# The front of a conformer, RWKV-7 and feed-forward layer: TensorE's order written out, and the output products of the two branches exchanged

## The chip, the core and the metric

The kernel runs on one core of one Trainium2 chip. TensorE (PE, with the weight loads PEld) multiplies, VectorE (DVE), ScalarE (ACT) and GpSimd (POOL) work on whole tiles, and SyncE (SP) issues the DMAs. The metric is the device time of one execution in microseconds, and lower is better. The profile is that of one execution.

## The reference

A layer with D = 1024 channels and T = 512 positions. One input product feeds three parts: a conformer convolution, an RWKV-7 recurrence with 16 heads of 64, and two gates.

```
h = modulate(rms_norm(x, g_norm1), shift1, scale1)        # shift, scale, gate: silu(c) @ w_ada
u_conv, u_rwkv, u_gate = split(h @ w_in)
z = depthwise_conv31(za * sigmoid(zb)); y_conv = silu(layer_norm(z)) @ w_pw + b_pw
u = u + mix * (u_prev - u); r, k, v, xw, xa, xg = split(u)
decay = exp(-exp(w_log(tanh(xw) @ w2)));  a = sigmoid(a0 + xa @ a2);  kk = normalised(k * k_k)
scan:  S = S * decay + (S @ -kk) (kk * a)^T + v k^T;  y = S @ r
y_rwkv = ((group_norm(y) + bonus(r, k, v)) * g) @ w_o
x = x + gate1 * ((g_conv * y_conv + g_rwkv * y_rwkv) @ w_out)
out = x + gate2 * (relu(modulate(rms_norm(x)) @ w_ff1)**2 @ w_ff2)
```

## The kernel before

**Dense blocks.** Everything is held with channels on partitions and the 512 positions along a tile. A large product goes by blocks of 128 output channels. `wload` brings the 512 KB of weights (`raw`), ACT casts them to a high part `wH` (L215), POOL makes the low part `wL = raw - wH` (L216), and the block is 24 matmuls of 128x512: for each of 8 chunks of the contraction wH by the high activations, wH by the low ones, wL by the high ones (L223, L224, L225). `raw`, `wH` and `wL` have two buffers each, and the accumulators `mm` three. The front has 52 blocks of `w_in` (k, r and v of the 8 RWKV blocks, six pairs for the convolution, 16 gates), then 8 of `w_pw` and 8 of `w_o`; `w_out` and the two feed-forward products come after and are not touched.

**RWKV.** The 16 heads go in four groups of two blocks (four heads). A group has these parts:
- `group_k` and `group_prep`: from k the low-rank products `pw`/`pa`, the norms `ss`/`rn`, the decay's exponentials `Pt` and `Pi` (L606, L610, behind an activation-table load), `decay_k` (the row norms spread by PE in `prn`, the normalised k `kkn`, kkn·a and the corrected k `kp`, both made by POOL but for two blocks, and `BK`), then r and v, and `products` (transposes `bkt`, Gram products `pG`, the masked `G` of L666, the values `UV`).
- `group_solve`: 31 dependent steps on DVE, each a product `tm` and a sum `Y` (L721, L723), with copies by ACT ahead (L712) and transposes behind (L729, L731); `group_solve2` finishes it on PE (`sW`, `sX`).
- `group_chain`: 8 steps that depend on one another. In each PE gives `ch<-S,AR` and `ch<-UV,G` (L767, L769), ACT copies F (L772), PE gives `ch<-F,G` (L776), ACT and DVE copy one half of UV each (L778, L779), PE gives `ch<-UV,bkT` (L784), and DVE makes `sp` and the next state `S` (L791, L792). Products `Y` (L799, L801) go beside it.
- `group_post`: the group norm of Y and its output.

**Convolution.** Each of 8 channel blocks is 31 weighted sums, one on ACT and 30 on DVE (L145, "taps" below), some 240 taps of 128x512.

**What sets the order.** The program is written part after part, and the scheduler issues by priority. The table `FORWARD` moves the priority of a section by a number of steps for each group, `WINDOWS` says which convolution and gate blocks are programmed around a group's solve, `after_dense` and `amid` tie small products to the last dense block or to a place in it, and `conv_taps` of later blocks may issue from the end of the solve. So each dense matmul goes where the priorities and ready times of the scheduler's model put it. Behind the front the norm of the convolution is programmed in the last group's window, `silu` behind it, then the `w_pw` blocks, then the `w_o` blocks.

## Time and profile before

| | |
|---|---|
| median of 3 runs | 1145.9 us (1145.41 to 1153.32) |
| profiled execution | 1150.57 us, span of the trace 1148.8 us |
| mean granted TensorE clock | 0.969 of full speed |
| busy share of the span | PE 93%, PEld 71%, DVE 67%, ACT 43%, POOL 37% |
| instructions | PE 6290, DVE 1145, ACT 805, POOL 237 |

A busy PE is a PE with matmuls in flight: the small products of a chain count as busy for their whole latency, so 93% says little of what the front could give. The stages of the front are told apart by the starts of `sW` (end of a group's solve) and the end of the chain.

### The profile page before, as it was taken

What the parts mean: (1) busy time and instruction counts of PE and PEld (TensorE: products, weight loads), DVE (VectorE), ACT (ScalarE), POOL (GpSimd) and SP (SyncE); (2) the same over time, 40 slices, a digit from 0 to 9 for tenths busy, and PEclk for the clock granted to TensorE, in tenths of its full rate; (3) what the DMA queues carried; (4) which work ended last, traced back from release to release, by engine and by line L of the source; (5) the groups of instructions that cost most, each with busy time, mean ns of one, the idle gap of its engine ahead of it and who ended that gap; (6) DMA issues with size and microseconds to landing.
All of it is one profiled execution on the core that took longest, in us unless ns stands there. A gap on an engine that the chain in (4) does not pass through costs nothing.

```text
span 1148.8 us, 16008 instructions
## 1 busy us (share of the span) xinstructions
PE 1066.7 (93%) x6290; PEld 818.6 (71%) x6290; DVE 765.2 (67%) x1145; ACT 494.8 (43%) x805; POOL 429.5 (37%) x237
## 2 busy tenths in 40 slices
PE   6898999998799989999979999998999999999997
PEld 5675776666566767667656777886888888888886
DVE  5878787789877898688845649788613612522545
ACT  5555534646155473365566412334413322422331
POOL 4744242243222334125431234453444444444441
PEclk9999799998899999999978999999999999999998
DMA  9622142112321125112636779952333333333332
GB/s 321 217 71 69 47 138 75 51 52 73 99 91 51 42 69 175 48 47 65 202 106 195 232 243 335 284 158 67 92 95 107 93 92 94 107 93 92 98 101 76
DMA packets 188922, 136.73 MB, mean 119 GB/s; under 512 B 5424, under 2 KB 162480, under 8 KB 188848
## 3 DMA queue, kind: packets, MB, share of 16 engines
q1 hardware_dynamic: 188848, 135.73, 38.4%
q8 instruction: 49, 0.80, 0.3%
q14 instruction: 25, 0.20, 0.1%
HBM read 121.55 MB, written 14.16 MB: 118 GB/s over the span
## 4 chain that ended last, share of the span: by engine, by line
PE 65%; DVE 19%; ACT 6%; DMA 5%; issue 3%; POOL 2%; SPq 0%; DVEq 0%; ACTq 0%; POOLq 0%
PE mm L223 16%; PE mm L224 16%; PE mm L225 16%; DVE acc L145 4%; PE pG L663 2%; ACT wH L215 1%; PE Y L801 1%; DMA adaw<-in_w_ada_dram 1%; PE Y L799 1%; PE ch L767 1%; PE ch L776 1%; DVE t2k L251 1%; PE ch L784 1%; DVE t2k L1022 1%; POOL wL L216 1%
## 5 line engine op out<-in xcount | busy, mean ns | idle before, releaser
L216 POOL TENSOR_TENSOR wL<-raw,wH 128x1024 fp32r<-128x1024 f32 x142 | 341.7, 2406 | 592.9 <-ACT wH L215 503.6
L223 PE MATMUL mm<-b,wH 128*128 128x512 f32 x720 | 292.0, 406 | 4.1 <-ACT cv L516 2.9
L225 PE MATMUL mm<-b,wL 128*128 128x512 f32 x720 | 291.0, 404 | 3.7 <-POOL wL L216 2.9
L224 PE MATMUL mm<-b,wH 128*128 128x512 f32 x720 | 291.2, 404 | 2.2 <-DVE b L1032 2.1
L215 ACT CAST wH<-raw 128x1024 fp32r<-128x1024 f32 x142 | 149.1, 1050 | 290.7 <-PE mm L224 238.9
L145 DVE SCALAR_TENSOR_TENSOR acc<-z,vt,acc 128x512 f32<-128x512 f32 x232 | 173.1, 746 | 1.8
L223 PEld LDWEIGHTS mm<-b,wH 128*128 128x128 f32 x720 | 136.9, 190 | 36.4 <-issue 3.5
L225 PEld LDWEIGHTS mm<-b,wL 128*128 128x128 f32 x720 | 137.0, 190 | 36.0 <-POOL wL L216 3.7
L224 PEld LDWEIGHTS mm<-b,wH 128*128 128x128 f32 x720 | 137.0, 190 | 33.5 <-DVE b L1032 3.5
L224 PE MATMUL mm<-g,wH 128*128 128x512 f32 x328 | 128.2, 391 | 1.2 <-DVE g L1024 0.9
L223 PE MATMUL mm<-g,wH 128*128 128x512 f32 x328 | 128.4, 391 | 0.0
L225 PE MATMUL mm<-g,wL 128*128 128x512 f32 x328 | 127.8, 390 | 0.0
L1022 DVE TENSOR_TENSOR t2k<-t2k 128x512 f32<-128x512 f32 x32 | 73.1, 2288 | 57.7 <-ACT t2k L1019 57.4
L1066 DVE SCALAR_TENSOR_TENSOR x<-mm,cols,x 128x512 f32<-128x512 f32 x31 | 23.3, 751 | 114.3 <-PE mm L225 114.3
L224 PEld LDWEIGHTS mm<-g,wH 128*128 128x128 f32 x328 | 61.6, 188 | 15.4 <-DVE g L1024 2.2
L223 PEld LDWEIGHTS mm<-g,wH 128*128 128x128 f32 x328 | 61.6, 188 | 14.0 <-ACT g L1023 1.2
L225 PEld LDWEIGHTS mm<-g,wL 128*128 128x128 f32 x328 | 61.6, 188 | 12.7 <-issue 0.2
L1023 ACT CAST g<-t2k 128x512 fp32r<-128x512 f32 x32 | 19.8, 621 | 72.7 <-DVE t2k L1022 72.7
L663 PEld LDWEIGHTS pG<-AR,BK 64*128 64x128 f32 x256 | 27.2, 204 | 14.2 <-DVE G L666 4.9
L663 PE MATMUL pG<-AR,BK 64*128 64x128 f32 x256 | 32.3, 306 | 5.1 <-DVE G L666 2.0
L1024 DVE TENSOR_TENSOR g<-t2k,g 128x512 fp32r<-128x512 f32 x32 | 23.4, 736 | 19.9 <-ACT g L1023 19.9
L723 DVE TENSOR_TENSOR Y<-tm,Y 128x126 f32<-128x126 f32 (+22 forms) x124 | 31.8, 257 | 3.4
(292 smaller groups left out, 1538.8 us busy)
## 6 DMA issues: line engine op xcount, KB each, us to landing
raw<-in_w_ff_dram SPq DMA_DIRECT2D x64, 512.0 KB, 4.1
raw<-in_w_in_dram SPq DMA_DIRECT2D x54, 512.0 KB, 3.7
adaw<-in_w_ada_dram SPq DMA_DIRECT2D x10, 1024.0 KB, 7.0
t2k<-gate SPq DMA_DIRECT2D x24, 256.0 KB, 3.8
adac<-in_w_ada_dram SPq DMA_DIRECT2D x24, 256.0 KB, 3.4
wa<-in_w_ada_dram SPq DMA_DIRECT2D x11, 512.0 KB, 5.3
gate<-cv SPq DMA_DIRECT2D x16, 256.0 KB, 2.2
raw<-in_w_pw_dram SPq DMA_DIRECT2D x8, 512.0 KB, 4.2
```

Source lines behind the costliest of these rows:

```text
L145: dve.scalar_tensor_tensor(dst if i == n - 1 else so_far, row, col, so_far, ALU.mult, ALU.add)
L215: act.copy(wH, raw)
L216: last_low[0] = pool.tensor_tensor(wL, raw, wH, ALU.subtract)
L223: steps.append(pe.matmul(acc, wH[:, kc, :], aH(kc), start=kc == 0, stop=False))
L224: steps.append(pe.matmul(acc, wH[:, kc, :], aL(kc), start=False, stop=False))
L225: steps.append(pe.matmul(acc, wL[:, kc, :], aH(kc), start=False, stop=kc == KC - 1))
L663: pe.matmul(pgs[e][:, i, :], BK[64 * e:64 * e + 64, c, C * e:C * e + 2 * C], G.AR[64 * e:64 * e + 64, b, c, :], start=True, stop=True)
L723: dve.tensor_tensor(X[:, s + 1:32, 0:w], tv, X[:, s + 1:32, 0:w], ALU.add)
L1022: dve.tensor_tensor(t, t, t, ALU.mult)
L1023: act.copy(rH(f), t)
L1024: dve.tensor_tensor(rL(f), t, rH(f), ALU.subtract)
L1066: dve.scalar_tensor_tensor(x1(j), acc, ada[:, 40 + j:41 + j], x1(j), ALU.mult, ALU.add)
```

## The change

The priorities leave the front. Every matmul of the front is pinned in program order (`pin`, on PE alone), and dense blocks are generators in a `queue`: `fill(n)` issues the next n dense matmuls at that place, and `need(name)` issues until a block is complete. The constants are `STAGE` (4 dense matmuls between the products of a chain step), `BELOW` (8 behind `sW` and in step 0) and `STEPS` (one tap for each two solve steps). Taps are placed by `tap(n)`: at most one for two solve steps, two for each chain step.

Within a group, the next group's low-rank product, norms with all four exponentials, and `decay_k` of both blocks are written inside chain steps 0, 1, 4 and 5; the parts of AR, the transposes, the Gram products and the group norm come behind the chain. POOL makes kkn·a and kp for all blocks (before, DVE did for blocks 3 and 5) and the convolution's running sum for all. The Y products are issued in each step, not for two steps together.

In the end of the front the `w_o` blocks now come first, with the convolution's norm inside them, and the `w_pw` blocks second. All computation stays. The diff, cut:

```diff
-WINDOWS = ("ccgg|g", "ccggg|", "cc|gggg", "ggg|ggg")
...
-PREP_AT = (0, 6)
-SOLVE_AT = (1, 13, 13, 13)
-NORM_AT, NORM_STEP = 63, 9
-POST_AT = 5
...
+WINDOWS = ("cccckk|rrgg", "vvcccckk|rrgg", "vvcccckk|rrgg", "vvggggg|ggggg")
...
+STAGE, BELOW, STEPS = 4, 8, 2
...
+    queue, ready, zs = [], {}, [None] * KC
+    anchor = [None]
...
+    def pin(i):
+        return tc.keep_in_program_order(i)
...
+    def block(c0, done):
+        wH, wL, raw = wload(w_in, 0, c0)
...
+                pin(pe.matmul(acc, a_[:, kc, :], b_(kc), start=kc == n == 0, stop=end))
+                if end:
+                    done(acc)
+                yield
...
+    def fill(n):
+        while n and queue:
+            name, gen = queue[0]
+            if next(gen, gen) is gen:
+                ready[name] = True
+                queue.pop(0)
+            else:
+                n -= 1
...
+    def need(name):
+        while name not in ready:
+            fill(1)
...
+    def tap(n=1):
...
+                    with tc.issue_after(anchor[0]):
+                        got = next(taps_left[0], 0)
...
+    def norms(G):
...
+    def decay_k(G, b):
+        p, k, a = G.blocks[b], G.k[b], G.a[b]
...
+        dve.scalar_tensor_tensor(kkn, k, V("k_k", p), prn, ALU.mult, ALU.mult)
+        BK = G.BK[b] = atile("BK", (P, NCH, 3 * C), 2)
+        ka = t2k()
+        pool.tensor_tensor(ka, kkn, a, ALU.mult)
+        dve.tensor_tensor(BK[:, :, C:2 * C], r3(ka), r3(G.Pi[b]), ALU.mult)
+        act.activation(a, a, AF.Identity, scale=V("k_a", p), bias=ka1[:, p:p + 1])
+        kp = G.kp[b] = t2k()
+        pool.tensor_tensor(kp, k, a, ALU.mult)
+        dve.tensor_tensor(BK[:, :, 0:C], r3(kp), r3(G.Pi[b]), ALU.mult)
+        act.copy(BK[64:128, :, 2 * C:3 * C], BK[64:128, :, 0:C])
...
+    def mul_ar(G, b):
...
+        dve.scalar_tensor_tensor(G.AR[:, b, :, 0:C], r3(G.kkn[b]), -1.0, G.Pt[b][:, :, 0:C], ALU.mult, ALU.mult)
+        dve.tensor_tensor(G.AR[:, b, :, C:2 * C], r3(r), G.Pt[b][:, :, 1:], ALU.mult)
+        dve.scalar_tensor_tensor(r, r, V("r_k", p), G.kp[b], ALU.mult, ALU.mult)
...
+    def products(G):
+
+        for b in range(NB):
+            need(("r", G.blocks[b]))
+            mul_ar(G, b)
...
+            anchor[0] = dve.tensor_tensor(X[:, s + 1:32, 0:w], tv, X[:, s + 1:32, 0:w], ALU.add).ins
+            if s % STEPS == STEPS - 1:
+                tap()
...
             act.copy(Fs, pf)
+            if c in between:
+                between[c]()
+            fill(STAGE if c else BELOW)
...
             dve.tensor_copy(G.UV[0:64, :, c, 1, :], pu[0:64])
+            fill(STAGE)
...
+            if c % 2 == 0:
                 py = psum("Y", 1, (P, NB, 2, C))
...
+            tap(2)
...
-            group_solve(G)
-        win = WINDOWS[g].split("|")
...
+        solve, chain = WINDOWS[g].split("|")
+        Gn = group(g + 1) if g < 3 else None
+        enqueue(solve, G, Gn)
+        group_solve(G)
+        tap(4)
+        if g:
+            need(("v", G.blocks[1]))
+        fill(12)
+        for b in range(NB):
+            values(G, b)
...
+        if post:
+            next(post, 0)
...
+        if g < 3:
+            need(("k", Gn.blocks[0]))
+            low_rank(Gn, 0)
+            tap(4)
+            need(("k", Gn.blocks[1]))
...
+        enqueue(chain, G, Gn)
+        fill(4)
+        group_solve2(G)
...
+        between = {}
+        if g < 3:
+            between = {0: lambda: low_rank(Gn, 1), 1: lambda: norms(Gn), 4: lambda: decay_k(Gn, 0), 5: lambda: decay_k(Gn, 1)}
+        Y = group_chain(G, between)
+        post = group_post(g, G, Y)
+        if g < 3:
+            products(Gn)
+            next(post)
...
+    for j in range(KC):
+        gt = t2k(tag="cv", bufs=2)
+        nc.sync.dma_start(gt, gate_d[8 + j])
+        acc = dense(w_o, 0, j * P, yH, yL)
+        dve.tensor_tensor(gt, acc, gt, ALU.mult)
+        nc.sync.dma_start(gate_d[8 + j], gt)
+        if j == 1:
...
+            act.activation(mean, pm, AF.Copy, scale=1.0 / D)
+            for i in range(KC):
+                ct8.append(t2k())
+                nc.sync.dma_start(ct8[i], conv_d[i])
...
+        if j in (2, 3, 4, 5):
...
+        if j == 6:
...
+            for i in range(KC):
+                t = ct8[i]
+                dve.tensor_tensor(t, t, plr, ALU.mult)
+                act.activation(t, t, AF.Silu, scale=V("ln_g", i), bias=V("ln_b", i))
+                act.copy(cH(i), t)
+                dve.tensor_tensor(cL(i), t, cH(i), ALU.subtract)
...
     for j in range(KC):
-        gt, m1 = gate_out(8 + j), gate_out(j)
-        acc = dense(w_o, 0, j * P, yH, yL)
-        dve.tensor_tensor(gt, acc, gt, ALU.mult)
+        gt, m1 = gate_out(j), gate_out(8 + j)
+        acc = dense(w_pw, 0, j * P, cH, cL)
+        dve.scalar_tensor_tensor(gt, acc, V("b_pw", j), gt, ALU.add, ALU.mult)
```

PE, a chain step of the first group. Dense matmuls are `mm` (L223 to L225 before, L521 after), the step is the `ch` products and `Y` its outputs. Before:

```order
L799 MATMUL Y_1690<-Sd_641,AR_764 64x128
L223 MATMUL mm_1881<-b_459,wH_1877 128x512
L776 MATMUL ch_1645<-F_1643,G_767 64x64 x4
L224 MATMUL mm_1881<-b_461,wH_1877 128x512
L225 MATMUL mm_1881<-b_459,wL_1878 128x512
L801 MATMUL Y_1690<-UV_765,G_767 64x64
L223 MATMUL mm_1881<-b_459,wH_1877 128x512
L224 MATMUL mm_1881<-b_461,wH_1877 128x512
L225 MATMUL mm_1881<-b_459,wL_1878 128x512
L223 MATMUL mm_1881<-b_459,wH_1877 128x512
L784 MATMUL ch_1652<-UV_765,bkT_766 64x64 x4
L801 MATMUL Y_1690<-UV_765,G_767 64x64
```

and after the change:

```order
L521 MATMUL mm_1640<-b_461,wH_1636 128x512
L521 MATMUL mm_1640<-b_459,wL_1637 128x512
L521 MATMUL mm_1640<-b_459,wH_1636 128x512
L521 MATMUL mm_1640<-b_461,wH_1636 128x512
L828 MATMUL ch_1737<-F_1731,G_1004 64x64 x4
L521 MATMUL mm_1640<-b_459,wL_1637 128x512
L521 MATMUL mm_1640<-b_459,wH_1636 128x512
L521 MATMUL mm_1640<-b_461,wH_1636 128x512
L521 MATMUL mm_1640<-b_459,wL_1637 128x512
L837 MATMUL ch_1751<-UV_1197,bkT_980 64x64 x4
L852 MATMUL Y_1711<-Sd_629,AR_965 64x128
L854 MATMUL Y_1711<-UV_1197,G_1004 64x64 x2
```

Before, one dense matmul stood in the first gap and six in the second; now each gap has four, and the Y products stand behind the step's last product.

ACT, the exponentials of the second group (`Pt`, and a `t2k` beside it for Pi) in the first group's chain. F and UV are the chain's copies. Before:

```order
L586 ACT_TABLE_LOAD
L586 ACTIVATE rn_1988<-ss_1873 128x256
L806 COPY Sd_639<-S_1758 64x2x64 x2
L772 COPY F_1787<-ch_1778 128x128
L606 ACT_TABLE_LOAD
L606 ACTIVATE Pt_1998<-t2k_1921 128x8x64
L778 COPY UV_765<-ch_1789 64x2x64
L610 ACTIVATE t2k_2002<-t2k_1921 128x512
L606 ACTIVATE Pt_2005<-t2k_1972 128x8x64
L610 ACTIVATE t2k_2009<-t2k_1972 128x512
```

and after:

```order
L821 COPY F_1606<-ch_1597 128x128
L654 ACT_TABLE_LOAD
L654 ACTIVATE rn_1617<-ss_1608 128x256
L663 ACT_TABLE_LOAD
L663 ACTIVATE Pt_1622<-t2k_1406 128x8x64
L664 ACTIVATE t2k_1624<-t2k_1406 128x512
L663 ACTIVATE Pt_1628<-t2k_1554 128x8x64
L664 ACTIVATE t2k_1630<-t2k_1554 128x512
L830 COPY UV_1197<-ch_1645 64x2x64
L856 COPY Yt_1533<-Y_1588 128x256
```

Both table loads and all four exponentials now stand between one step's F and UV copies; before, one load and one exponential did.

DVE, the second group's `decay_k` against the first group's chain (UV, sp and S are the chain's; L145 before is a tap). Before:

```order
L779 COPY UV_765<-ch_1818 64x2x64
L145 SCALAR_TENSOR_TENSOR acc_1361<-z_455,vt,acc_1361 128x512
L620 SCALAR_TENSOR_TENSOR t2k_2050<-kk_1874,vt,prn_2045 128x512
L145 SCALAR_TENSOR_TENSOR acc_1361<-z_455,vt,acc_1361 128x512
L621 SCALAR_TENSOR_TENSOR AR_1992<-t2k_2050,Pt_1998 128x8x64
L145 SCALAR_TENSOR_TENSOR acc_1361<-z_455,vt,acc_1361 128x512
L625 TENSOR_TENSOR BK_2053<-t2k_2050,t2k_2002 128x8x64
```

and after:

```order
L673 SCALAR_TENSOR_TENSOR t2k_1791<-kk_1380,vt,prn_1786 128x512
L677 TENSOR_TENSOR BK_1793<-t2k_1794,t2k_1624 128x8x64
L831 COPY UV_1197<-ch_1813 64x2x64
L844 TENSOR_TENSOR sp_1830<-ch_1824,S_1756 128x128
L681 TENSOR_TENSOR BK_1793<-t2k_1798,t2k_1624 128x8x64
L845 TENSOR_TENSOR S_1829<-sp_1830,PC_834 128x128
```

Before, `decay_k` began behind the chain's last UV copy, among taps; now kkn and the first BK stand ahead of step 4's UV copy, and the second BK ahead of its state S. Both BK wait for a POOL product.

## Rows read from the trace of the kernel before

**Rows 1.** The page, the chain that ended last: share of the span by engine.

```profile
PE 65%; DVE 19%; ACT 6%; DMA 5%; issue 3%; POOL 2%; SPq 0%; DVEq 0%; ACTq 0%; POOLq 0%
```

**Rows 2.** Dense matmuls by stage: stretch, length, busy (count), PEclk, DMA share, GB/s.

```profile
70.70:173.20 102.50, 75.20 (x295) 0.93 0.30 89
173.20:234.00 60.80, 35.80 (x114) 1.00 0.20 61
234.00:321.60 87.60, 56.63 (x209) 0.90 0.27 83
321.60:380.20 58.60, 33.04 (x104) 1.00 0.18 56
380.20:453.40 73.20, 55.23 (x218) 1.00 0.31 97
453.40:515.60 62.20, 37.07 (x119) 1.00 0.20 60
515.60:597.20 81.60, 54.24 (x192) 0.94 0.38 125
597.20:651.00 53.80, 28.90 (x86) 0.87 0.62 198
651.00:729.00 78.00, 70.23 (x299) 1.00 0.85 276
860.00:1120.00 260.00, 259.31 (x1140) 1.00 0.34 97
```

**Rows 3.** Timeline of PE, one step of the last chain: start, us, instruction, [idle].

```profile
635.09 0.34 PE L767 MATMUL ch<-S,AR 64*64 64x64 f32 x4
...
640.24 0.28 PE L767 MATMUL ch<-S,AR 64*64 64x64 f32 x2
```

**Rows 4.** Timeline of ACT in the first group's chain.

```profile
219.12 1.28 ACT L606 ACT_TABLE_LOAD   x1
220.41 0.63 ACT L606 ACTIVATE Pt<-t2k 128x512 f32<-128x512 f32 x1
221.07 0.26 ACT L778 COPY UV<-ch 64x128 f32<-64x128 f32 x1
```

**Rows 5.** Timeline of DVE: two solve steps' parts, then the first group's chain.

```profile
160.95 0.29 DVE L721 TENSOR_TENSOR tm<-s,Y 128x126 f32<-128x126 f32 x1
161.28 0.29 DVE L723 TENSOR_TENSOR Y<-tm,Y 128x126 f32<-128x126 f32 x1
...
187.53 0.75 DVE L145 SCALAR_TENSOR_TENSOR acc<-z,vt,acc 128x512 f32<-128x512 f32 x1
188.19 0.29 DVE L792 TENSOR_TENSOR S<-sp,PC 128x128 f32<-128x128 f32 x1
...
226.07 1.23 DVE L792 TENSOR_TENSOR S<-sp,PC 128x128 f32<-128x128 f32 x1
```

**Rows 6.** Timeline of POOL in the first group's chain and behind it.

```profile
224.75 2.40 POOL L216 TENSOR_TENSOR wL<-raw,wH 128x1024 fp32r<-128x1024 f32 x1 [1.99 <-ACT wH L215]
232.83 1.28 POOL L624 TENSOR_TENSOR t2k<-t2k,t2k 128x512 f32<-128x512 f32 x1 [5.68 <-DVE AR L621]
```

**Rows 7.** DVE from 70 to 680 by line: out<-in xcount | busy, mean ns | idle before.

```profile
L666 DVE TENSOR_TENSOR G<-pG,ct 128x512 f32<-128x512 f32 x32 | 21.5, 682 | 5.4 <-PE pG L663 5.3
L792 DVE TENSOR_TENSOR S<-sp,PC 128x128 f32<-128x128 f32 x24 | 15.0, 624 | 0.1
L640 DVE TENSOR_TENSOR AR<-t2k,Pt 128x512 f32<-128x512 f32 x8 | 8.9, 1109 | 0.0
L729 DVE STREAM_TRANSPOSE s<-s 128x1024 f32<-128x1024 f32 x4 | 8.6, 2138 | 0.1
```

**Rows 8.** ACT from 70 to 680 by line.

```profile
L712 ACT COPY s<-G 32x512 f32<-32x512 f32 x32 | 18.4, 615 | 10.1 <-DVE G L666 9.8
L626 ACT ACTIVATE t2k<-t2k,cols,vt 128x512 f32<-128x512 f32 x8 | 6.5, 815 | 13.2 <-POOL t2k L624 13.2
L938 ACT ACTIVATE t2k<-t2k,vt 128x512 f32<-128x512 f32 x8 | 6.4, 811 | 0.1
```

More of the change, by code (lines that the diff above doesn't have):

```diff
@@ new lines, in set_z, with taps @@
+    def set_z(p, z):
+        def taps():
+            o = csum if p == 0 else t2k(tag="co", bufs=1)
+            terms = [(z[:, j:j + T], V("conv_w", p * TAPS + j)) for j in range(TAPS)]
+            yield from weighted_steps(o, terms, V("conv_b", p))
+            nc.sync.dma_start(conv_d[p], o)
+            if p:
+                pool.tensor_tensor(csum, csum, o, ALU.add)
+        taps_left.append(taps())
+    taps_left = []
+    def tap(n=1):
+        for _ in range(n):
+            while taps_left:
+                if anchor[0] is None:
+                    got = next(taps_left[0], 0)
+                else:
+                    with tc.issue_after(anchor[0]):
+                        got = next(taps_left[0], 0)
+                if got != 0:
+                    break
+                taps_left.pop(0)
@@ L592, in group_prep @@
[L592 to L603 removed]
+        G.g, G.blocks = g, [g * NB + b for b in range(NB)]
@@ new lines, in group, with k_block, done @@
+        G.k, G.a, G.sg, G.sq, G.r, G.v, G.vb = ([None] * NB for _ in range(7))
+        G.Pt, G.Pi, G.BK, G.kkn, G.kp, G.bonus = ([None] * NB for _ in range(6))
+        return G
+    def k_block(G, b):
+        def done(acc):
+            p = G.blocks[b]
+            G.k[b] = t2k(tag="kk", bufs=2)
+            shifted(acc, G.k[b], 8 + p)
+            G.sq[b] = t2k()
+            act.activation(G.sq[b], G.k[b], AF.Square, scale=V("k_k", p))
+        return ("k", G.blocks[b]), block(R0 + D + G.blocks[b] * P, done)
@@ new lines, in values @@
+    def values(G, b):
+        if b == 0:
+            G.UV = atile("UV", (P, NB, NCH, 2, C))
+        v, p = G.v[b], G.blocks[b]
+        pv = pmisc((P, 4, 2, C), "pv")
+        for i in range(4):
+            pin(pe.transpose(pv[:, i].rearrange("p e t -> p (e t)"), v[:, i * P:(i + 1) * P], ident))
+        for par in range(2):
+            for e in range(2):
+                act.copy(G.UV[64 * e:64 * e + 64, b, par::2, e, :], pv[64 * par:64 * par + 64, :, e, :])
+        rH, rL = G.bonus[b]
+        pb = pmisc(name="bonus")
+        pin(pe.matmul(pb, blkr, rH, start=True, stop=False))
+        pin(pe.matmul(pb, blkr, rL, start=False, stop=True))
+        dve.tensor_tensor(v, pb, v, ALU.mult)
+        nc.sync.dma_start(vb_d[p], v)
@@ L872, in tile_block @@
         pool.memset(t, 0.0)
-    with forward("k", 0):
-        G = group_k(0)
-    group_prep(0, G)
-    for g in range(4):
-        with forward("solve", g):
-            group_solve(G)
-        win = WINDOWS[g].split("|")
-        lnb = 3 if g == 3 else 1
-        for i in range(lnb):
-            with forward("window", g):
-                window(win[0][i:i + 1])
-            if i == 0:
-                with after_dense():
-                    group_bonus(g, G, 1)
-        if g == 3:
-            with forward("norm"):
-                steps = sum(dense_log[-lnb:], [])
+    G = group(0)
@@ new lines, in tile_block @@
+    queue += [f(G, b) for f in (k_block, r_block, v_block) for b in range(NB)]
+    fill(62)
+    pcol = pmisc((P, 4), "pcol")
+    for i in range(4):
+        pin(pe.matmul(pcol[:, i:i + 1], reds[i], ones[:, 0:1], start=True, stop=True))
+        fill(3)
+    ecol = cols[:, 112:116]
+    act.copy(ecol, pcol)
+    for p in range(2):
+        act.activation(eacc[2 * p], eacc[2 * p], AF.Sigmoid, bias=ecol[:, 2 * p:2 * p + 1])
+        za = eacc[2 * p + 1]
+        dve.scalar_tensor_tensor(za, za, ecol[:, 2 * p + 1:2 * p + 2], eacc[2 * p], ALU.add, ALU.mult)
+        set_z(p, zp[p])
@@ new lines, in tile_block @@
+    next(post)
+    fill(30)
+    next(post, 0)
+    while queue:
+        fill(1)
+    tap(200)
+    stC = ExitStack()
+    cpool = stC.enter_context(tc.tile_pool(name="convh", bufs=1))
+    yal = lambda dt: cpool.tile([P, 4, T], dt, name=nm("c8"), tag="c8", bufs=4)
+    yH, yL = pair(yal), pair(yal)
+    for j in range(KC):
+        if j < 6:
+            t = t2k()
+            nc.sync.dma_start(t, yo_d[j])
+        else:
+            t = G.vb[j - 6]
+        act.copy(yH(j), t)
+        dve.tensor_tensor(yL(j), t, yH(j), ALU.subtract)
```

469 lines of the change are left out of this document (190 added, 279 removed).

## The prediction

> **What bounds the kernel now.** I read the chain of the work that ended last first. PE has 65% of it and DVE 19% [rows 1], so most of the span is matmuls one behind another, and DVE's share has to lie where PE has nothing to do. Behind the front it has not: from 860 to 1120 us PE gives 1140 dense matmuls in 260 us, 0.228 us each [rows 2], and that is the floor of a dense matmul at full clock. So the change can only win or lose in the front, and there I read the dense matmuls by stage. The cuts are the start of `sW` (the end of a group's solve) and the end of each chain: the nine stages are solve and chain in turn, for four groups, and the end of the front. For each I take its length less 0.228 us for each dense matmul in it. What is left, the rest, is what small products, waits and a lower clock cost. In order: 35.2, 34.8, 39.9, 34.9, 23.5, 35.1, 37.8, 34.2 and 9.8 us, together 285 us of 658 [rows 2]. For example the first chain is 60.8 - 114 x 0.228 = 34.8.
>
> Two things set the rest. In a chain a step cannot be shorter than its own latency: the leanest step of the trace goes from 635.09 to 640.24, 5.15 us, with seven dense matmuls in it [rows 3], while the mean step of the first three chains takes (60.8 + 58.6 + 62.2) / 24 = 7.6 us [rows 2]. In the solve stages DVE has its 62 instructions one behind another, a product starting at 160.95 and its sum at 161.28, 0.33 us apart [rows 5].
>
> **The change part by part.** The dense matmuls are the same, so I add up the rests. The counts of dense matmuls are those of the new order: 292 up to the first `sW`, 76 in each chain, 212 between a chain and the next `sW` (188 for the last group), 424 in the end.
>
> *The solve's path* in the new order, from the last mask: eight copies by ACT of 0.615 us = 4.9 [rows 8]; a transpose of 2.1 [rows 7]; 62 x 0.33 = 20; fifteen taps and some eight other 512-wide instructions among the steps; and 4 us at the end (a copy, a transpose as above, and a shuffle estimated at half of one). A tap takes 0.66 us of DVE's time when something stands behind it (187.53 to 188.19) [rows 5], and none where the pair had a gap; between 0 and 0.66 I take 0.57, near the measured end, as the solve's steps leave almost no gap: 13 us. Together 44 to 45 us; with free taps 32.
>
> *Stage 1.* Behind the products PE has 148 dense matmuls, 34 us, and some 4 us of small ones: 38 us against the solve's 45, so it waits 7 us. The earlier part of the stage I leave as it is; its written order has the same products in the same order. Rest +7; with free taps 0.
>
> *The first three chains.* A base step has eight dense matmuls against seven in the lean step of before, whose latency covers them: 5.0 us, as I take a little less for the Y products moved out of the gaps. Solve2 and the start 6, step 0 with the low-rank product and its two sigmoids on ACT 7. Step 1: ACT has both table loads, the square root and all four exponentials between F and UV. In the trace the load took 1.28 us and an exponential 0.63, and one load and one exponential stood ahead of a UV copy [rows 4]. Now 2 x 1.28 + 4 x 0.63 and the root, 5.4 us, stand where four dense matmuls and the F product (1.8 us) cover: +3.4 to +3.6, 8.4 us. Steps 4 and 5: DVE has kkn (0.75, the price of a tap), then waits for POOL's product of 1.28 us [rows 6], then BK of 0.68 (as a mask of that size [rows 7]), and only then UV: 3.1 us against 1.8 of cover, +1.3. Then sp, and S is behind the second BK, which waits for ACT's 0.815 us [rows 8] and POOL's other 1.28: +1.0. With a little for S, +2.7: 7.7 us each. The last step has no state, 3.5. So 6 + 7 + 8.4 + 2 x 5.0 + 2 x 7.7 + 5.0 + 3.5 = 55.3. S also loses time to POOL: its mean was 0.624 us against 0.29 undisturbed [rows 5, 7]; 0.34 x 6 = 2. So 57 us with 76 dense matmuls, a rest of 39.7: against 104.8 for three, +14.3. Queued behind the waiting instructions are only DVE's own taps and ACT's weight casts (`wH`), for which PE has two buffers.
>
> *The last chain* has no next group, only five taps in a step, whose 3.3 us fit in the step's gaps in part. I take 49 us, a rest of 31.7: -2.5.
>
> *Products and solve of groups 1 and 2.* Behind the chain DVE is alone at work: two AR parts and the weighted r for two blocks (0.7 to 1.1 each [rows 7]), 5.4; eight masks of 0.68 [rows 7], 5.5; four passes of the group norm over 1024 columns at twice a mask's price less a little, 5. So 16 us in which PE has 16 dense matmuls. Then PE has 196 x 0.228 = 44.7 and some 7 us of small products, 52 us, against the solve's 45: PE sets the pace, which before it did not. With 1.5 us for clock (these stages had 0.90 and 0.94 of it at times [rows 2]) 69.5 us and a rest of 21.2, where it was 39.9 and 23.5: -21. Group 3 alike, with 172: 16 + 46.5 = 62.5, a rest of 19.6 against 37.8: -18.2. This is the gain of the change. If the taps cost more than 0.57 it falls, since the solve's path passes PE's 52 at 0.9 us a tap.
>
> *The end of the front.* `w_o` needs the last group's post, and the norm of the convolution now lies among its blocks: eight squares on ACT at the price of its copy, 0.615 us [rows 8], some 5 to 6 us with PE's sums. Then eight times silu and cast, (0.811 + 0.615) x 8 = 11.4 us [rows 8], have one `w_o` block of 24 x 0.228 = 5.5 us ahead of the first `w_pw` block: some 5 us of wait. Before, the last chain covered this. +10.5, a rest of 20.3 in place of 9.8. If the cover were complete it would be 0.
>
> SP's queue moves as well: the stores of `yo`, `gate` and the loads of `conv` change places, but DMA was busy 0.18 to 0.38 of the time in the first seven stages and 0.62 to 0.85 in the last two [rows 2], and the loads that made the 0.85 only come later. I take nothing for it. It would cost up to the 1.5 us or so of a late weight load per block if these met `wload`.
>
> Sum: 7 + 14.3 - 2.5 - 21 - 18.2 + 10.5 = -9.9. The profiled execution took 1150.6 and would take 1140.7; the median, 4.7 below it, goes from 1145.9 to **1136 us**. The bounds of the parts: free taps and covered silu give -7 and -10.5 more, ACT and DVE work hidden in the chains -26 (D), the POOL delays +15 to +29 (B, C).
>
> **The rivals.** *A, the forecast,* 1136: spread 1124 to 1148 by the taps' price and the clock.
>
> *B, POOL's products hold the chain's DVE instructions.* Two blocks of `decay_k` in three chains bring 12 POOL products of 1.28 us [rows 6] into the steps. An S took 1.23 us at 226.07 [rows 5] while POOL's `wL` ran from 224.75 to 227.15 [rows 6]; it ended as that ended. If each POOL product holds one chain instruction for its whole length, 12 x 1.28 = 15 more: 1151, no change. For it: that row. Against it: S's mean of 0.624 [rows 7] says that most are not held, and DVE waits for most of these products anyway.
>
> The Trainium skill has this rule ("SBUF — State Buffer", section "SBUF: two separate sides"): a GpSimd instruction and a VectorE one with both inputs in SBUF share one pair of ports, which the first takes for the whole instruction. By that rule the price of B is the right one. The trace agrees for S at 226.07, which has both inputs in SBUF.
>
> *C, slower.* The same 12 products stand in POOL's queue among the weights' `wL`, and a `wL` takes 2.40 us [rows 6]. In written order PE's next block is always near, so a `wL` is likely to run when kkn comes. If each product waits for one, UV or S is late by 2.4 each time: 12 x 2.4 = 29, 1165 us. It decides (more than 1% slower, 1157) from 9 of the 12. Against it: POOL was idle 1.99 and 5.68 us ahead of the two rows [rows 6], and busy for 37% only.
>
> *D, faster.* The exponentials and `decay_k` don't extend the steps: dense matmuls, Y products and steps overlap so that 5.0 holds everywhere. That takes away 3.4 + 2 x 2.7 a chain, 26 us: 1110. For it: the mean step of before held such work too, at 7.6 us with half as many dense matmuls again. Against it: on ACT the four exponentials now stand in one piece ahead of UV, and an engine takes its instructions in the order it has them.
>
> **How the numbers follow.** About 1% is what a measurement of this kernel can tell from no change, here 1134 and 1157 us. A 0.40, B 0.18, C 0.16, D 0.26. The range that holds 8 in 10 leaves out the outer half of C and D: 1106 to 1163. A alone is 1124 to 1148. Faster: D and nearly half of A, 0.26 + 0.18 = 0.44. The same: the other half of A and most of B, 0.22 + 0.13 = 0.35. Slower: C and the rest of B, 0.21.
>
> **What would show it.** In the profile after, the time from one `sW` to the next shows the parts. The chain's steps: 5 us for steps 2, 3 and 6, 8.4 for step 1 with ACT's exponentials between F and UV, 7.7 for steps 4 and 5 with DVE waiting on POOL. From the end of a chain to `sW`: 16 us with little PE and then 52 with PE full; if PE waits for `s` of the solve there, the taps were priced too low. In the end a wait of the first `w_pw` block for the cast of silu, of some 5 us. The prediction is wrong if step 1 takes 5 us (then D), if steps 4 and 5 take over 10 (then C), or if the stages of the feed-forward product, which I hold at 0.228 us a matmul, move.

## The result

The changed kernel takes 1182.5 us (1182.1 to 1187.6, four runs) where the kernel before took 1148.7 in the same runs: a ratio of 1.030, interval 1.025 to 1.035. It is 34 us slower; 1136 was forecast. The profiled execution has a span of 1180.9 us.

The page's busy times hardly move: PE has the same work, in a longer span.

```profile
PE 1066.9 (90%) x6290; PEld 845.6 (72%) x6290; DVE 757.4 (64%) x1140; ACT 493.2 (42%) x804; POOL 437.1 (37%) x242
```

The dense matmuls of the changed kernel by stage, cut as in [rows 2]: stretch, length, busy (count), PEclk, DMA share, GB/s. The last row goes on to the norm behind `w_out`, since the two ends of the front hold different numbers of blocks.

```profile
70.70:187.80 117.10, 74.50 (x295) 0.86 0.27 80
187.80:247.00 59.20, 23.88 (x76) 0.93 0.11 33
247.00:315.30 68.30, 51.77 (x212) 1.00 0.33 100
315.30:374.00 58.70, 23.25 (x77) 0.91 0.14 39
374.00:444.90 70.90, 53.09 (x212) 0.98 0.30 93
444.90:504.30 59.40, 23.96 (x77) 0.91 0.14 43
504.30:569.70 65.40, 48.19 (x189) 0.95 0.45 147
569.70:624.00 54.30, 23.81 (x77) 0.94 0.31 101
624.00:817.60 193.60, 161.50 (x643) 0.96 0.70 220
```

For the kernel before the last stretch up to the same place is this:

```profile
651.00:782.80 131.80, 119.75 (x513) 1.00 0.78 245
```

Again the length less 0.228 us for each dense matmul is the rest of a stage. Against [rows 2]:

| part | rest before | rest after | change | forecast |
|---|---|---|---|---|
| stage 1 | 35.2 | 49.8 | +14.6 | +7 |
| first three chains | 104.8 | 124.8 | +20.0 | +14.3 |
| last chain | 34.2 | 36.7 | +2.5 | -2.5 |
| products and solve, groups 1 and 2 | 63.4 | 42.6 | -20.8 | -21 |
| the same, group 3 | 37.8 | 22.3 | -15.5 | -18.2 |
| end of the front | 14.8 | 47.0 | +32.2 | +10.5 |
| sum | | | +33.0 | -9.9 |

So the signs were right but for the last chain, and the gain came nearly as forecast (36.3 of 39.2 us). The costs did not: the end is 22 us worse than forecast, stage 1 8 us, the chains 11 us.

**A chain step, after.** ACT in the first chain (start, us, instruction): both table loads and all four exponentials stand between F at 202.53 and UV at 208.02, as the order said. UV can't be copied before that, and the step lasts from 201.18 to 210.82.

```profile
202.53 0.27 ACT L821 COPY F<-ch 128x128 f32<-128x128 f32 x1
202.82 1.28 ACT L654 ACT_TABLE_LOAD   x1
...
204.51 1.28 ACT L663 ACT_TABLE_LOAD   x1
205.81 0.63 ACT L663 ACTIVATE Pt<-t2k 128x512 f32<-128x512 f32 x1
...
208.02 0.26 ACT L830 COPY UV<-ch 64x128 f32<-64x128 f32 x1
```

DVE in step 4 of the same chain, with its idle time and the releaser at the end of the row: BK waits for POOL's first product ahead of UV, the second BK for the other one ahead of S.

```profile
225.58 0.75 DVE L673 SCALAR_TENSOR_TENSOR t2k<-kk,vt,prn 128x512 f32<-128x512 f32 x1 [0.52 <-PE prn L671]
227.72 0.69 DVE L677 TENSOR_TENSOR BK<-t2k,t2k 128x512 f32<-128x512 f32 x1 [1.39 <-POOL t2k L676]
228.33 0.28 DVE L831 COPY UV<-ch 64x128 f32<-64x128 f32 x1
...
229.92 0.69 DVE L681 TENSOR_TENSOR BK<-t2k,t2k 128x512 f32<-128x512 f32 x1 [0.46 <-POOL t2k L680]
230.53 0.28 DVE L845 TENSOR_TENSOR S<-sp,PC 128x128 f32<-128x128 f32 x1
```

The starts of `ch<-S,AR` on PE (each row a step's first) give the steps: 9.64 us for step 1, 6.00 for 2, 6.94 for 3, 7.20 and 7.26 for 4 and 5, 4.54 for 6. In the other two chains they are much alike, but for 8.54 in step 4 of the second and 4.56 in step 3 of the third.

```profile
201.18 0.34 PE L816 MATMUL ch<-S,AR 64*64 64x64 f32 x4
...
210.82 0.49 PE L816 MATMUL ch<-S,AR 64*64 64x64 f32 x4
...
216.82 0.34 PE L816 MATMUL ch<-S,AR 64*64 64x64 f32 x4 [0.44 <-DVE S L845]
...
223.76 0.34 PE L816 MATMUL ch<-S,AR 64*64 64x64 f32 x4 [2.33 <-DVE S L845]
...
230.96 0.34 PE L816 MATMUL ch<-S,AR 64*64 64x64 f32 x4 [0.94 <-DVE S L845]
...
238.22 0.34 PE L816 MATMUL ch<-S,AR 64*64 64x64 f32 x4 [0.94 <-DVE S L845]
...
242.76 0.34 PE L816 MATMUL ch<-S,AR 64*64 64x64 f32 x4
```

**The clock.** PE by stretch (stretch, length, busy and instructions, PEclk, DMA share, GB/s). In the products of the first group the queue holds no more blocks, `fill` issues nothing, and PE does next to nothing from 117 to 122. The granted clock then stands at 0.50, the lower of its two levels (1.2 GHz), up to 143, while the Gram products run (0.43 us each in the mean, 0.31 over the trace of before). The same happens where PE waits 5.2 us for the first solve, ahead of `sW` at 187.8. The kernel before has one such stretch, at 0.50 from 120 to 127.

```profile
117.00:122.00 5.00, 0.77 (x6) 0.88 0.00 0
122.00:126.00 4.00, 3.59 (x16) 0.50 0.08 21
126.00:131.00 5.00, 0.57 (x3) 0.50 0.30 88
131.00:143.00 12.00, 11.64 (x55) 0.50 0.00 0
182.60:187.80 5.20, 0.41 (x2) 0.80 0.20 58
187.80:194.60 6.80, 6.53 (x136) 0.65 0.12 36
```

The first Gram product waits for AR, a product of DVE:

```profile
122.41 3.75 PE L713 MATMUL pG<-AR,BK 64*128 64x128 f32 x16 [4.63 <-DVE AR L688]
```

Before, it started at 117.77. The changed kernel makes this AR on DVE at 121.58, behind the four BK of both blocks, each of which waits for POOL, and the taps between them; before, AR of the first block stood at 106.5 and 107.5, ahead of its BK.

**The end.** All of PE's instructions from the end of the last chain to the norm behind `w_out`, before and after (columns as under the clock):

```profile
651.00:782.80 131.80, 127.05 (x590) 1.00 0.78 245
```

```profile
624.00:817.60 193.60, 173.37 (x799) 0.96 0.70 220
```

With the dense rows above, this divides the +32.2 us: PE is idle 20.2 us in place of 4.8 (+15.5); the dense matmuls take 14.9 us more than 0.228 us each, in place of 2.8 (+12.1); small products take the other 4.6. Of the idle time PE waited 4.9 us for silu's low part, 4.8 for a `wL`, 3.7 for a `wH` and 3.6 for a modulation sum.

DVE among the `w_o` blocks: the results of a block (`cv`, L1026) stand in DVE's order behind the modulation sums, and these wait for 256 KB pieces (`adac`), 14.3 us in all. Whether PE loses time by it is read in e12.

```profile
665.82 0.69 DVE L1026 TENSOR_TENSOR cv<-mm,cv 128x512 f32<-128x512 f32 x1 [2.72 <-DMA adac<-in_w_ada_dram]
...
673.44 0.75 DVE L137 SCALAR_TENSOR_TENSOR acc<-adac,cols,acc 128x512 f32<-128x512 f32 x1 [5.27 <-DMA adac<-in_w_ada_dram]
```

All engines in two stretches of the `w_pw` blocks (busy and instructions of PE, PEld, DVE, ACT, POOL; PEclk, DMA share, GB/s): the DMA engines are full and PE is not.

```profile
724.00:734.00 10.00, 7.26 (x30) 5.66 (x29) 8.84 (x14) 2.06 (x3) 2.39 (x1) 0.72 0.94 315
734.00:744.00 10.00, 5.16 (x18) 3.30 (x16) 5.15 (x8) 2.51 (x3) 2.16 (x1) 0.84 0.95 304
```

A full DMA alone does not hold PE. In the kernel before (the row has PE's columns only) it is as full, with PE busy throughout:

```profile
700.00:710.00 10.00, 10.00 (x54) 1.00 1.05 340
```

### The profile page after: what moved, and what is told of

The parts are those of the page before. It is cut to its first block, busy times and chain, and to the rows that moved or that the text cites. A ratio compares the mean times of both kernels' runs of the same rounds, so it can differ in the third digit from the quotient of the medians.

```text
span 1180.9 us, 16020 instructions
## 1 busy us (share of the span) xinstructions
PE 1066.9 (90%) x6290; PEld 845.6 (72%) x6290; DVE 757.4 (64%) x1140; ACT 493.2 (42%) x804; POOL 437.1 (37%) x242
## 5 line engine op out<-in xcount | busy, mean ns | idle before, releaser
L521 PE MATMUL mm<-b,wH 128*128 128x512 f32 x832 | 282.1, 413 | 0.0
L521 PEld LDWEIGHTS mm<-b,wH 128*128 128x128 f32 x832 | 160.4, 196 | 36.6 <-issue 3.8
L521 PE MATMUL mm<-b,wL 128*128 128x512 f32 x416 | 172.5, 415 | 0.6 <-POOL wL L217 0.6
L225 PE MATMUL mm<-g,wH 128*128 128x512 f32 x328 | 128.2, 391 | 1.1 <-DVE g L1123 0.9
L225 PE MATMUL mm<-b,wH 128*128 128x512 f32 x304 | 120.4, 397 | 6.6 <-DVE b L1056 4.9
L224 PE MATMUL mm<-b,wH 128*128 128x512 f32 x304 | 120.6, 398 | 4.0 <-ACT wH L216 3.7
L521 PEld LDWEIGHTS mm<-b,wL 128*128 128x128 f32 x416 | 81.4, 196 | 18.9 <-issue 1.2
L225 PEld LDWEIGHTS mm<-b,wH 128*128 128x128 f32 x304 | 58.2, 191 | 20.7 <-DVE b L1056 6.1
L225 PEld LDWEIGHTS mm<-g,wH 128*128 128x128 f32 x328 | 61.6, 188 | 15.3 <-DVE g L1123 2.2
L224 PEld LDWEIGHTS mm<-b,wH 128*128 128x128 f32 x304 | 58.3, 192 | 17.4 <-ACT wH L216 4.5
L226 PEld LDWEIGHTS mm<-b,wL 128*128 128x128 f32 x304 | 58.1, 191 | 15.0 <-POOL wL L217 3.1
L713 PE MATMUL pG<-AR,BK 64*128 64x128 f32 x256 | 40.2, 326 | 12.9 <-DVE G L715 5.1
```

What stands on the lines that cost most here:

```text
L224: steps.append(pe.matmul(acc, wH[:, kc, :], aH(kc), start=kc == 0, stop=False))
L225: steps.append(pe.matmul(acc, wH[:, kc, :], aL(kc), start=False, stop=False))
L226: steps.append(pe.matmul(acc, wL[:, kc, :], aH(kc), start=False, stop=kc == KC - 1))
L521: pin(pe.matmul(acc, a_[:, kc, :], b_(kc), start=kc == n == 0, stop=end))
L713: pin(pe.matmul(pg[:, i, :], G.BK[b][64 * e:64 * e + 64, c, C * e:C * e + 2 * C], G.AR[64 * e:64 * e + 64, b, c, :], start=True, stop=True))
```

## The experiments

For all kernels I cut the front in three: 70.7 to the first `sW` (start), to the last `sW` (middle: three chains, three products and solves), and to the norm behind `w_out` (last). The number is the rest, length less 0.228 us per dense matmul. Each line is one profiled execution, in e5 and e8 the slowest of its kernel's runs, in e1, e7 and e9 the fastest. Kernels whose start part is the same code differ there by up to 4 us, and so do those with the same last part (80.8 to 84.4), so that much is no effect.

| kernel | median us | start | middle | last |
|---|---|---|---|---|
| before | 1150 | 35.2 | 206.5 | 48.7 |
| changed | 1182.5 | 49.8 | 190.4 | 82.9 |
| e1 front of before, end of after | 1167.5 | 31.7 | 192.9 | 82.2 |
| e2 no taps in solve 1 | 1166.0 | 44.4 | 178.4 | 81.7 |
| e3 decay behind the state | 1190.5 | 48.7 | 199.2 | 84.4 |
| e4 exponentials split | 1171.6 | 52.5 | 175.6 | 84.4 |
| e5 weights ahead of gates | 1178.7 | 52.0 | 193.3 | 80.7 |
| e6 = e2 + e4 | 1157.1 | 44.2 | 172.5 | 80.8 |
| e7 decay's products on DVE | 1179.7 | 52.0 | 185.2 | 81.8 |
| e8 e6, e5, more taps, norm earlier | 1178.0 | 46.9 | 206.4 | 66.8 |
| e9 e6, products filled | 1163.4 | 41.6 | 175.2 | 80.8 |
| e10 e6, e5, e7, norm earlier | 1152.7 | 45.7 | 170.5 | 75.2 |
| e11 no norm, no silu | 1175.2 | 48.7 | 190.1 | 76.5 |
| e12 one load per sum | 1173.3 | 49.8 | 190.8 | 70.9 |
| e13 state in PSUM | 1171.5 | 49.9 | 185.4 | 77.5 |
| e14 = e10 + e13 | 1146.9 | 44.8 | 169.6 | 70.5 |

The kernel before, run beside each group, had medians of 1149.2 to 1150.5.

**e1: the exchanged end alone.** `before`, with the norm taken out of the last group's window, the last `group_post` ahead of the blocks, and the end of the changed kernel.

> The front of the kernel before, with only its end exchanged: the norm of the convolution inside the w_o blocks, w_o first and w_pw second. Theory 1 (the exchanged end is what costs: silu, the norm and late weights stand where the last chain used to cover them): the rest of the end grows by 25 to 30 us, the last solve and chain give back some 5 us of the norm that they held, so 1168 to 1174 us. Theory 2 (the end is slow only because the front of the changed kernel delivers the convolution late): at most 1153 us.

1167.5 us, ratio 1.016 (1.014 to 1.019). The three parts of the dense matmuls (columns as above):

```profile
70.70:168.70 98.00, 72.43 (x291) 0.98 0.31 90
168.70:579.10 410.40, 266.34 (x954) 0.98 0.28 87
579.10:798.80 219.70, 153.45 (x603) 0.91 0.62 194
```

The last part rests 82.2 us, as in the changed kernel, with the scheduler's front ahead of it: +33.5, where 25 to 30 were expected, of which the middle gives back 13.6, all of it between the third chain and the fourth `sW`: the norm that left the last solve. So the exchange costs some 17 us net, half of the loss, with either front. It also says that the middle's gain of 16 us in the changed kernel is nearly all the norm leaving; the written order itself gains only some 2 us there, the solves' gain and the chains' loss being equal.

**e2: no taps in the first solve,** four for six steps in the others in place of three.

```diff
-            if s % STEPS == STEPS - 1:
+            if G.g and s % 3 != 2:
```

> The changed kernel with no taps in the first group's solve, and four for each six steps in place of three in the others. Theory (15 taps lengthen the first solve, and PE has nothing to do meanwhile): the first solve takes 37 us in place of 44.7, the other stages stay, 1174 to 1176 us. Rival (PE's wait there is not from the taps, or the taps put into the other solves cost as much): 1180 to 1184 us.

1166.0 us, 16.5 less than the changed kernel, twice the forecast. The start gives 5.4 us of the 7.7 that were sized, since PE's own work now lasts to `sW`, but the middle gives 12 more. With the solve ready in time PE no longer waits ahead of `sW`, its clock stays at 1.00 there, and the first chain begins 4.3 us behind `sW` in place of 6.8, of which its step 0 takes back 0.8. The six taps more in each of the other solves were free: PE waits ahead of no `sW`. The largest piece of the 12 us is luck: in the third chain a `w2L` of DVE that `wL` had held (1.66 us) now takes 0.29, and from `sW` to step 1 it is 10.9 us in place of 15.7. The rest was not taken apart.

**e3: `decay_k` behind the state** of steps 4 and 5, not ahead of UV.

```diff
-            if c in between:
+            if c in between and c < 4:
                 between[c]()
...
+            if c in between and c >= 4:
+                between[c]()
             tap(2)
```

> The changed kernel with decay_k written behind the state of chain steps 4 and 5, not ahead of their UV copy. Theory (DVE's UV copy and S stand behind BK, which waits for POOL): steps 4 and 5 take 5.3 us in place of 7.2, three chains, 1170 to 1173 us. Rival (the delay only moves to the next step, or into the products behind the chain): 1180 to 1184 us.

1190.5 us, slower. Steps 4 and 5 do shrink, to 5.64 and 6.10 us, but step 6 grows from 4.54 to 7.70:

```profile
224.76 0.34 PE L816 MATMUL ch<-S,AR 64*64 64x64 f32 x4 [2.32 <-DVE S L845]
...
230.40 0.34 PE L816 MATMUL ch<-S,AR 64*64 64x64 f32 x4
...
236.50 0.34 PE L816 MATMUL ch<-S,AR 64*64 64x64 f32 x4
...
244.20 0.49 PE L816 MATMUL ch<-S,AR 64*64 64x64 f32 x4 [2.56 <-DVE S L845]
```

The second BK, waiting for POOL, now stands ahead of the next step's sp. The three steps together take 19.4 in place of 19.0 us: the wait was moved, not removed. The middle is 8.8 us longer all the same; 6.4 of that lie behind the chains of the first two groups, up to the next `sW`, and 3.6 at the start of the first chain.

**e4: the exponentials split,** two behind the UV copy of step 2, two behind that of step 3, each held by `issue_after`; the square root behind that of step 1.

```diff
-            between = {0: lambda: low_rank(Gn, 1), 1: lambda: norms(Gn), 4: lambda: decay_k(Gn, 0), 5: lambda: decay_k(Gn, 1)}
+            between = {0: lambda: low_rank(Gn, 1), 1: lambda: norms(Gn), 2: lambda: exps(Gn, 0), 3: lambda: exps(Gn, 1), 4: lambda: decay_k(Gn, 0), 5: lambda: decay_k(Gn, 1)}
...
+        with tc.issue_after(hold[0] or G.sqrt.ins):
```

> The changed kernel with the four exponentials not together ahead of step 1's UV copy on ACT: the square root behind the UV copy of step 1, two exponentials behind that of step 2, two behind that of step 3. Theory (ACT's 5.4 us of loads and exponentials between F and UV lengthen step 1): step 1 takes 6 us in place of 9.6, steps 2 and 3 at most 0.5 more, three chains, 1172 to 1175 us. Rival (DVE's reciprocal and taps hold that step as long): 1180 to 1184 us.

1171.6 us, 11 less, all of it in the middle (-15, the start being 2.7 longer). In the second chain step 1 goes from 10.13 (326.13 to 336.26) to 5.88 us:

```profile
328.74 0.34 PE L820 MATMUL ch<-S,AR 64*64 64x64 f32 x4
...
334.62 0.34 PE L820 MATMUL ch<-S,AR 64*64 64x64 f32 x4 [0.65 <-DVE S L851]
...
339.68 0.34 PE L820 MATMUL ch<-S,AR 64*64 64x64 f32 x4 [0.44 <-DVE S L851]
```

Step 2 takes 5.06 there, and the third chain's step 1 falls alike, to 5.77. The theory on ACT's order holds in these two. In the first chain step 1 still takes 8.80: S stands there behind DVE's reciprocal of the norms (1.74 us), as the rival had it.

**e5: a block's weights ahead of its gate loads** in the `w_pw` loop.

```diff
+        w = wload(w_pw, 0, j * P)
         gt, m1 = gate_out(j), gate_out(8 + j)
-        acc = dense(w_pw, 0, j * P, cH, cL)
+        acc = wmul(w, cH, cL)
```

> The changed kernel with one line in the w_pw loop moved: the load of a block's weights is issued ahead of the two gate loads of that block, not behind them. Theory (gate loads wait for free buffers in SP's queue and hold the weights behind them; PE waited 4.1, 2.0 and 0.9 us for wH and wL around 737 to 744, and ran at half clock around it): 1171 to 1177 us. Rival (the DMA engines are full there, 0.95 of the time, and the weights come no earlier): 1180 to 1184 us.

1178.7 us (1174.5 to 1184.5): between the two. The last part falls by 2.2 us, within the spread of that part, so no effect of this order of loads is shown.

**e6: e2 and e4 together.**

> The changed kernel with both edits that shortened it alone: no taps in the first solve, and the exponentials split behind the UV copies of steps 1 to 3. Theory (the two have separate places): the gains of 16.5 and 11 us add up, 1153 to 1158 us. Rival (both gave the same thing back, PE's full clock behind a wait): 1160 to 1168 us.

1157.1 us (1156.6 to 1157.6): in the time the two nearly add up, 25.4 us against 16.5 and 10.9. In the parts they do not: the start gives 5.6, as in e2, but the middle 17.9, where e2 and e4 alone gave 12.0 and 14.8. Step 1 of the second and third chains takes 8.8 us, against 5.9 and 5.8 in e4, since the reciprocal now stands ahead of S on DVE there too:

```profile
321.88 1.75 DVE L656 RECIPROCAL rn<-rn 128x256 f32<-128x256 f32 x1
...
324.12 0.28 DVE L851 TENSOR_TENSOR S<-sp,PC 128x128 f32<-128x128 f32 x1
```

e10 and e14 carry this step as well (8.7 to 8.8 us).

**e7: the two products of `decay_k` on DVE** (`dve.tensor_tensor` for `pool.tensor_tensor`).

> The changed kernel with the two products of decay_k on DVE for all blocks, as blocks 3 and 5 had them before. Theory (in steps 4 and 5 the way from DVE to POOL and back holds UV and S): 0.7 us instead of 1.3 for each product and two hand-overs less, steps of 6.0 in place of 7.2 us, 1173 to 1177 us. Rival (what holds them is DVE's order, kkn and BK ahead of UV): steps of 7 us, 1180 to 1184 us.

1179.7 us. Steps 4 and 5 fall to 6.1 us, as the theory has it, and the middle by 5; in the time 2.8 us are left, within the spread of the start.

**e8: e6 and e5, a tap behind each step of solves 1 to 3, the norm one `w_o` block earlier.**

```diff
-        if j == 1:
+        if j == 0:
             with after_dense():
                 pm = pmisc(name="mean")
```

> The two edits of the exponentials and the first solve, the weights ahead of the gate loads, a tap behind every step of the other three solves so that the convolution ends within the last chain, and the norm of the convolution one w_o block earlier, so that two w_o blocks stand behind silu's start. Theory (the end is slow because the convolution ends late and one block of 5.5 us covers silu's 11.4): the end's rest falls from 46 to about 32 us, 1137 to 1145 us. Rival (the end is bound by its loads, whatever the norm's place): 1150 to 1156 us.

1178.0 us: against e6 the last part falls by 14 us to 66.8, as forecast, and the middle rises by 34. With 31 taps a solve takes longer than PE's work beside it, and PE waits 16.3 us ahead of these three `sW`, where in e6 it waits for none; the rest of the 34, in the chains' starts and steps, was not taken apart. Taps are not free beyond the point that PE's work sets.

**e9: the first group's products filled** with two convolution blocks, eight dense matmuls at each place (on e6).

> The kernel with the two edits on taps and exponentials (1157 us), and besides 48 dense matmuls of the first two convolution blocks put between the first group's transposes and Gram products, eight at each place, in place of the empty queue there. Theory (PE waits 5.1 and 4.9 us for AR and the masks, its granted clock falls to 0.50 from 122 to 145 us, and the Gram products behind it run at half speed): the clock stays at 1.00 and the first stage shortens by 5 to 8 us, 1149 to 1152 us. Rival (DVE's AR and masks set the pace there, the clock costs nothing): 1156 to 1159 us.

1163.4 us (1157.3 to 1169.1), not faster; the parts are those of the fastest run. The start gains 2.6 us, and the middle loses as much: the same dense matmuls are then missing beside the solve, PE idles 6.3 us ahead of `sW`, and the chain begins 6.8 us behind it, at 0.68 of the clock. The clock did not stay at 1.00 in the products either (0.50 from 125 to 135), and the last mask came 4.0 us later than in e6. The edit moves the hole, and does not show what the clock costs there.

**e10: e6, e5, e7 and the norm one block earlier,** taps as in e6.

> The kernel with the edits on taps and exponentials (1157 us), besides the weights ahead of the gate loads (-3.8), decay_k's products on DVE (-2.8), and the convolution's norm one w_o block earlier, with the taps where the changed kernel had them. Theory (two blocks of w_o cover silu): the end's rest falls by 11 us as it did when the taps were moved too, 1137 to 1143 us. Rival (without earlier taps the norm only waits in the first w_o block): 1148 to 1152 us.

1152.7 us, ratio 1.002 (1.000 to 1.005). Against e6 the last part falls by 5.6 us, half of the forecast, and the time is next to the rival's range; why not by more was not taken apart.

**e11: the convolution's norm and silu left out.**

> The changed kernel with the convolution's norm and silu left out (mean, squares, root and silu are not computed; the w_pw product takes the convolution as it is, cast two chunks in each of the blocks 2 to 5), to read what they cost where they now stand. Theory (silu ahead of the first w_pw block, the norm's sums and POOL's eight subtractions ahead of a wL make most of the end's loss): the end's rest falls from 46 to 27 to 32 us, 1164 to 1169 us. Rival (the loads and the modulation sums make it): a rest of 40 or more, 1176 to 1182 us.

1175.2 us. The last part falls by 6.4 us only, from 82.9. The rival is nearer: what the prediction named as the end's cost is a fifth of it.

**e12: one load for each modulation sum.**

```diff
-            wa = alloc(n)
-            nc.sync.dma_start(wa, w_ada[kc * P:(kc + n) * P, c0:c0 + 512].rearrange("(k p) c -> p k c", p=P))
+            if kc == 0 or n > 1:
+                wa = alloc(n)
+                nc.sync.dma_start(wa, w_ada[kc * P:(kc + n) * P, c0:c0 + 512].rearrange("(k p) c -> p k c", p=P))
```

> The changed kernel with the modulation sums of the end (256 KB pieces, eight to a sum) reading their first piece eight times, so that 21 of 24 loads of the end are left out and DVE's work stays. Theory (the pieces come late, DVE waits for them in its order with the w_o results behind, and the weights share their queue): the end's rest falls from 46 to 30 to 36 us, 1168 to 1174 us. Rival (the loads are hidden, and the end's loss is that the last chain and post no longer cover w_pw blocks): rest above 42, 1178 to 1183 us.

1173.3 us, and the last part falls by 12.0, as the theory sized it, but not by its way. I count the dense matmuls from the fourth `sW` on. The 385th starts 150.3 us behind it in the changed kernel and 151.0 us in e12: up to there, past the `w_o` blocks and all of DVE's waits for `adac`, nothing is gained. The 457th starts at 182.7 and 170.7: the whole gain lies in these 72 matmuls of the `w_pw` blocks, 20 us behind the issue of the last of these loads (699.51). PE over them, in the changed kernel and in e12 (stretch, length, busy and instructions, PEclk, DMA share, GB/s):

```profile
720.00:752.40 32.40, 24.57 (x89) 0.79 0.91 299
```

```profile
721.30:741.00 19.70, 18.51 (x89) 1.00 0.92 308
```

The DMA share is the same, so a full DMA is not what PE loses here. In the changed kernel PE waits 2.5 us in it for the next modulation sum and 3.7 for a `wH`, and its clock falls. SP issued that sum's loads (`adaw`, 1 MB each) from 713.43, in e12 from 703.65, and weights behind them at 729.35, in e12 at 721.50. So the loads that were left out are the largest part of the end that a run told apart, and they seem to act through SP's order, on what it issues later; that was not tested alone.

**e13: sp made in place in PSUM,** on the changed kernel.

```diff
-                    sp = atile("sp", (P, NB, C))
-                    dve.tensor_tensor(sp, pn, S, ALU.add)
-                    dve.tensor_tensor(Sn, sp, pcb, ALU.mult)
+                    dve.tensor_tensor(pn, pn, S, ALU.add)
+                    dve.tensor_tensor(Sn, pn, pcb, ALU.mult)
```

> The changed kernel with the sum sp of the state made in place in PSUM, so that S has one input in SBUF and not two. Theory (S, with both inputs in SBUF, is held by a wL of POOL to its end; S took 0.51 us in the mean against 0.28, and four chain steps took 6.95 where 4.55 to 5.1 is the rest): 5 to 9 us less, 1173 to 1178 us. Rival (S is late because DVE's other instructions stand ahead of it): 1181 to 1184 us.

1171.5 us, 11 less, more than sized. The state's last product by line, in the changed kernel and in e13 (xcount | busy, mean ns | idle):

```profile
L845 DVE TENSOR_TENSOR S<-sp,PC 128x128 f32<-128x128 f32 x24 | 12.3, 514 | 0.1
```

```profile
L844 DVE TENSOR_TENSOR S<-ch,PC 128x128 f32<-128x128 f32 x24 | 6.8, 283 | 0.1
```

In the changed kernel four of the 24 were held (1.16, 1.16, 2.17 and 2.17 us, the others 0.3), in e13 none. That is the 5.5 us by which their own time falls, most of it in the last chain, whose two steps of 6.95 take 5.1; where the rest of the 11 comes from was not taken apart.

**e14: e10 and e13 together.**

> The combined kernel (1153 us) with sp made in place in PSUM. Theory: the last chain's two steps of 6.95 take 5.1, some 4 to 8 us less in all, 1145 to 1149 us, as fast as the kernel before or faster. Rival: 1151 to 1155 us.

1146.9 us, ratio 0.996 (0.994 to 0.998): a third of a per cent faster than the kernel before, and 36 us faster than the change. It is a balance: its last part still rests 22 us more than that of the kernel before, and its middle 37 us less.

## Why the prediction was wrong

**The end of the front (+10.5, measured +32).** This is the step that failed. It was priced by the instructions of the moved parts, norm 5 to 6 and silu 5 us. For these the price was enough: PE waited 4.9 us for silu's low part, as forecast, and e11 gets 6.4 us back for both. What it left out is what else lies there. "I take nothing for it", the sentence on SP's queue said, though it named 1.5 us per block as the price if loads met `wload`, which over 16 blocks is 24 us. In its place the trace shows +15.5 us of idle PE, +12.1 of dense matmuls slower than 0.228 us, with the clock at 0.72 to 0.84 around the longest waits, and +4.6 of small products. Before, 17 of the 24 small loads of the modulation sums were issued beside the last chain; now 22 come behind it, on the same queue as the weights. e12 gives 12 us to these loads, e11 6 to norm and silu, and e5 shows no effect of the gate loads. Some 14 us stay open. e1 shows that the loss belongs to the exchange and not to the front, and in e1 PE waited 9.5 us for the last group norm, which `w_pw` blocks covered before.

**Group 3's gain (-18, measured -15.5)** was the right size by luck, with the wrong reason. The prediction credited it to PE setting the pace; e1 has 13.6 of it with the scheduler's front, since it is the norm that left that solve. The same work was then underpriced where it went.

**Stage 1 (+7, measured +14.6).** The solve's path was right: 43.6 us from the last mask to `sW`, with 44 to 45 forecast, where the kernel before took 35.1. The step "the earlier part of the stage I leave as it is" failed, by 6.1 us: the last mask ends at 144.2 in place of 138.1. Its reason, "the same products in the same order", does not hold for DVE, where AR now stands behind the BK of both blocks; the first Gram product waits for it and starts 4.6 us later. PE has nothing else in its queue there, and its clock is at the lower level for 21 us. How much of the 6.1 us is DVE's order and how much the clock no run shows: in e9 the clock fell all the same.

**The chains (+14.3, measured +20; last chain -2.5, measured +2.5).** Step 1 was forecast at 8.4 and took 9.6 to 10.6. Steps 4 and 5, forecast at 7.7, took 7.2 to 7.3, and once 8.5. Steps 2 and 3 were forecast at 5.0; step 2 took 5.6 to 6.4, and step 3 in two of three chains 6.95: there S stands behind another instruction of DVE and is held by a `wL`. The third chain's step 0 took 11.4 us against 6.6 in the other two: a `w2L` of DVE was held 1.4 us by a `wL` in the same way, ACT then waited 3.5 us for DVE and PE 2.3 us for ACT, and the clock over these 10 us was 0.66. In the last chain two held S make steps of 6.95. e13 takes away the holds of S, not that of `w2L`. These holds are not why the change is slower: the kernel before had five held S of its own (1.2 to 2.4 us), the changed kernel four, and the forecast had 2 us for them in each of the first three chains.

**The solves of groups 1 and 2 (-21, measured -20.8)** are right, mechanism and size: PE-bound, PEclk 1.00 and 0.98.

**The rivals.** B (POOL holds DVE's chain instructions, 15 us) named the right mechanism and the wrong holder: not decay's products, for which DVE waits anyway, but `wL`. For one S of e10 the rows show it to the end of the `wL`:

```profile
573.38 2.17 DVE L851 TENSOR_TENSOR S<-sp,PC 128x128 f32<-128x128 f32 x1
```

```profile
573.06 2.34 POOL L217 TENSOR_TENSOR wL<-raw,wH 128x1024 fp32r<-128x1024 f32 x1 [12.65 <-ACT wH L216]
```

575.55 and 575.40 are the two ends. The Trainium skill ("SBUF — State Buffer", section "SBUF: two separate sides") states this: two SBUF inputs on VectorE against a GpSimd instruction that reads SBUF, the second one blocked for the whole of the first. The traces agree: 0.514 us in the mean against 0.283 with one input in PSUM. C (slower by 29 through decay's products behind `wL`) had the side right and not the place: steps 4 and 5 were as forecast. D (hidden) is excluded by e4: the exponentials were on the path.

The range failed because all its upper side was in the chains. The end had one bound, 0 to 10.5, and no case in which the loads make it.
